# First feed-forward by halves, three more modulation vectors on TensorE, and the first two products of a stage side by side

## The chip, the cores and the metric

One core of a Trainium2 chip. The metric is the device time of one execution in microseconds; the median of the kernel before is 2867.61 us over 3 runs (2865.7 to 2867.91).

## The reference

A stack of two layers over 512 tokens `x` and 256 context tokens `ctx`, all 1024 wide. Each layer is a feed-forward, a mixer and a second feed-forward, each with a modulation computed from a condition vector. The mixer of layer 0 is attention with compressed keys beside an mLSTM, that of layer 1 a gated linear recurrence (RG-LRU).

```python
def ada_params(cond, w, b):
    m = jax.nn.silu(cond) @ w + b
    return jnp.split(m, N_MOD, axis=-1)          # 9 vectors of 1024
def modulate(h, shift, scale):
    return h * (1.0 + scale) + shift
def swiglu(h, w_gate, w_up, w_down):
    return (jax.nn.silu(h @ w_gate) * (h @ w_up)) @ w_down     # 1024 -> 2816 -> 1024

for layer in range(2):
    mx, mc = ada_params(c, ...), ada_params(c_ctx, ...)
    x = x + 0.5 * mx[2] * swiglu(modulate(rms_norm(x), mx[0], mx[1]), w_gate, w_up, w_down)
    ctx = ctx + 0.5 * mc[2] * swiglu(modulate(rms_norm(ctx), mc[0], mc[1]), ...)
    x, ctx = x + mx[5] * y_x, ctx + mc[5] * y_c      # y: even or odd mixer of the modulated norm
    x = x + 0.5 * mx[8] * swiglu(modulate(rms_norm(x), mx[6], mx[7]), ...)
    ctx = ctx + 0.5 * mc[8] * swiglu(modulate(rms_norm(ctx), mc[6], mc[7]), ...)    # layer 0 only
```

## The kernel before

**Layout.** The activations stay transposed in SBUF as eight tiles `xT[k]` of 128 features by 768 columns (256 of the context, 512 of x). An fp32 product is made of three products of parts: high by high, high by low, low by high. `split_to` writes a tile's high part (`xh`, `ah`) on ScalarE and its low part (`xl`, `al`) on VectorE (L522). The class `Stream` (object `ws`) loads weights into `raw` buffers and splits them into `unit` buffers, ScalarE for the high part (L260), VectorE for the low part (L261); three units are live at once.

**Stages.** P[0] to P[5] are the six stages: feed-forward, even mixer, feed-forward (layer 0), feed-forward, odd mixer, feed-forward (layer 1, x alone). The text calls them the first to the sixth. A `Normed` stage multiplies by the rms factor R only after its product. `chunk(k)` makes the stage's input for 128 features: `scale` (ScalarE L551 for `xh`, VectorE L552 for `xl`), then `square`, which squares on ScalarE (L562) and adds to `acc` (L563). That add runs on GpSimd for k below `SQ` (8; in the sixth stage `SQ3`, 6), else on VectorE. `chunk` is called by the stage before as soon as its last down product has been accumulated into `xT[k]` (L741). `shifts` puts the shift vectors into four extra columns (L522, tiles of 128x4). `norm` multiplies `acc` by ones on TensorE (`nps`, L584 and L585, in halved stages L718 and L719) and takes the root: `rv`, ScalarE's sqrt, a reciprocal (L514) and a Newton step to `ry`.

**Feed-forwards.** The hidden width is 22 blocks of 128, the f-blocks. `gen_ffn`, of the first stage, makes for each f-block two whole products of 48 matmuls (8 chunks, 3 part products, tiles of 258 and 512 columns; L598). `gen_halved`, of the third, fourth and sixth, makes the first 4 f-blocks so (`whole`) and the other 18 by a scheme of halves (`halves`): seven products of 12 matmuls of 386 columns (L730), after sums and differences of weights (`Stream`) and of inputs (`widen`, `settle`) on VectorE. The down products (L782, halved L908) come in groups of f-blocks, `HG` = 4, 4, 4, 4, 3, 3, two outputs side by side. Both functions yield after each product or so, and at each yield a `fill` function is called.

**Modulation.** The 9 vectors of layer 0 are numbered 0 to 8. Those in `order` (1, 0, 2) are made on TensorE in 12 steps of 256 columns: `mod_step` issues the loads of the next step, `mod_mm` (8 matmuls with the weights moving, L366) and `mod_post` of the step before (two transposes L377, then VectorE). The other vectors of both layers are made by `mod_late` on VectorE: per 768 columns and chunk a multiply-add of 128x768 (L465) into `macc`, then a transpose, a reduce and four small matmuls (L441). `mod_some(n)` advances it n operations per yield: 6.3 in the first stage (`MF0`), 0.4 and 0.52 in the third and fourth. `mod_ready` makes what is still missing before its use.

**Order.** The Tile framework's scheduler fixes each engine's order from the program; by hand only the start and first products (`ordered(OS)`) and ScalarE's order in the odd mixer. Each engine works in its order.

**Product starts.** In `gen_halved` with no `first`, `whole(0)` makes the gate product, yields, calls `norm`, then makes the up product. In the odd mixer `values(0)` (V0) makes its product and the norm, then `branch(0)` (B0) its own; `proj_start` of the even mixer makes the product of the gates and then that of `v`, head 0.

Of the kernel before, what the change touches and what calls it, by code (L numbers as in the profile page):

```python
# [15 lines left out]
KD = 8  # L16
# [25 lines left out]
SQ = 8  # L42
# [7 lines left out]
SQ3 = 6  # L50
# [37 lines left out]
FL = 2  # L88
FS = 2
MF0 = 6.3  # L90
MF1 = 0.4
MF2 = 0.52
HG = [4, 4, 4, 4, 3, 3]
# [4 lines left out]
NPX = 4  # L98


ALL = [(0, 258, [(0, 0, 256, C)], 256), (258, 770, [(0, 256, 768, X)], None)]
XO = [(256, 514, [(2, 256, 512, X)], 0), (514, 770, [(0, 512, 768, X)], None)]
# [19 lines left out]
def tile_hybrid_block(  # L122
# [188 lines left out]
    ws = Stream()  # L311
# [33 lines left out]
    order = [(0, 4 * n + i) for n in (1, 0, 2) for i in range(4)]  # L345
# [65 lines left out]
    def mod_late():  # L411
# [3 lines left out]
        todo = [(l, g, b, k) for l, g in ((0, 1), (0, 2), (1, 0), (1, 1), (1, 2)) for b in range(4) for k in range(KD)]  # L415
# [77 lines left out]
    def mod_ready(l, n):  # L493
        while MS["left"][l, n]:
            if (l, n // 3) == (0, 0):
                mod_step()
            else:
                next(MS["late"])
# [25 lines left out]
    class Normed:  # L524
# [78 lines left out]
        def part(self, u, ps, i):  # L603

            a, b, _, _ = self.tiles[i]
            todo = [(k, n) for k in range(KD) for n in range(3)]
            if PO:
                todo.sort(key=lambda q: q[1])
            for k, n in todo:
                wi, src = ((0, self.h), (0, self.lo), (1, self.h))[n]  # L610
                mm(ps[:, 0:b - a], lhsT=u[:, wi, k, :], rhs=src[k][:, a:b], start=(k, n) == (0, 0), stop=(k, n) == (KD - 1, 2))

# [181 lines left out]
    def gen_halved(P, l, j, nxt, first=None, plain=NP, groups=HG):  # L794
# [27 lines left out]
        def whole(f):  # L822
            if f == 0 and first is not None:
                pg, pu = first
            else:
                pg = P.product(ws.next())
                yield
                if f == 0:
                    P.norm()
                pu = P.product(ws.next())  # L830
# [281 lines left out]
    def proj_start(P):  # L1112

        pss = P.product(ws.next(), 64)
        M["z"], M["turn"] = {}, [[], []]
        first = gen_proj(P, [("v", 0)])
        next(first)
# [700 lines left out]
    def odd_mixer(P, nxt):  # L1818
# [26 lines left out]

        def values(n):
            pz = steps()
            if n == 0:
                P.norm()
            bz = P.bias(pz)  # L1850
# [32 lines left out]
        def branch(n):  # L1883
            pg = steps(XO)
# [111 lines left out]
    add_ffn(0, 0)  # L1996
# [10 lines left out]
    P = [Normed(0, 0), Normed(0, 1), Halved(0, 2), Halved(1, 0), Normed(1, 1), Halved(1, 2, True)]  # L2007
# [50 lines left out]
    def fill():  # L2058
        MS["n"] = MS.get("n", 0) + 1
        if MS["n"] < FS:  # L2060
            pass
        elif MS["mm"] <= len(order):
            mod_step(FL)
        else:
            some_late()
# [6 lines left out]
    run(gen_ffn(P[0], 0, 0, P[1].chunk, pss), fill)  # L2072
# [67 lines left out]
```

## Time and profile before

| | us |
|---|---|
| median of 3 runs | 2867.61 |
| profiled execution | 2867.53 |
| its span | 2865.8 |
| TensorE busy | 2756.6 (96%) |
| VectorE busy | 2229.0 (78%) |
| ScalarE busy | 1096.7 (38%) |
| GpSimd busy | 263.8 (9%) |

The span is the time from the first to the last instruction; the rest of the execution's time lies around it. Busy time says how long an engine had something to do and nothing of how fast it ran: TensorE's clock is granted in two levels, and the mean granted clock of a stretch stands beside its busy times.

### The profile page before, as it was taken

The page shows a single profiled execution, that of the slowest core. Times are in us where ns is not written, and L with a number is a line of the kernel's source. Part 1 is how long each engine was busy: PE and PEld are TensorE (multiplying, and loading weights), DVE is VectorE, ACT ScalarE, POOL GpSimd, SP SyncE. Part 2 cuts the span into 40 slices and gives each one's busy share as a digit, 9 for nine tenths or more (in the row PEclk, how much of TensorE's full clock was granted, in tenths as well). Part 3 has the DMA queues.
Part 4 walks back from the last instruction along what each step waited for, and adds up shares of the span by engine and source line. Part 5 has one row for each costly group of instructions (what it writes and reads, how often), then busy time and mean ns, then how long its engine had stood idle before and what let it go on. Part 6 is the DMA issues. An engine that isn't in the chain of part 4 may idle for free.

```text
span 2865.8 us, 40947 instructions
## 1 busy us (share of the span) xinstructions
PE 2756.6 (96%) x16185; PEld 2453.1 (86%) x16185; DVE 2229.0 (78%) x3673; ACT 1096.7 (38%) x1743; POOL 263.8 (9%) x274
## 2 busy tenths in 40 slices
PE   6999999999999899899999999999999997899998
PEld 4888888888888677789999998999999886799997
DVE  5367767796765667878879897989887899888886
ACT  4212111234443456443223344323323475643433
POOL 1000000021342200100000010000000353100000
PEclk8999999999999899999999999999999998899999
DMA  7434333342443110123223232234322211223332
GB/s 208 124 114 133 119 128 125 122 141 54 139 146 107 55 58 31 52 77 100 87 83 107 89 95 72 91 116 147 133 92 71 58 57 49 85 82 103 100 101 87
DMA packets 356634, 282.00 MB, mean 98 GB/s; under 512 B 14665, under 2 KB 327226, under 8 KB 356442
## 3 DMA queue, kind: packets, MB, share of 16 engines
q1 hardware_dynamic: 353722, 266.02, 30.1%
q0 software_dynamic: 2720, 13.37, 1.3%
q8 instruction: 127, 2.08, 0.3%
q14 instruction: 65, 0.53, 0.1%
HBM read 263.78 MB, written 15.56 MB: 97 GB/s over the span
## 4 chain that ended last, share of the span: by engine, by line
PE 54%; DVE 9%; issue 1%; ACT 1%; DMA 1%; POOL 0%; SPq 0%; DVEq 0%; ACTq 0%
PE ps L730 24%; PE ps L908 16%; PE ps L598 8%; PE ps L1416 2%; DVE xl L552 2%; DVE unit L261 1%; DVE xT L741 1%; PE oacc L1633 1%; PE ps L1590 1%; PE ps L1621 1%; DVE U L1873 1%; PE ps L1900 1%; DVE I L1931 0%; DVE S L1936 0%; DVE S L1929 0%
## 5 line engine op out<-in xcount | busy, mean ns | idle before, releaser
L598 PE MATMUL ps<-xh,unit 128*128 128x258 f32 (+3 forms) x3328 | 727.4, 337 | 10.5 <-DVE unit L261 8.7
L260 ACT CAST unit<-raw 128x1024 fp32r<-128x1024 f32 (+3 forms) x338 | 333.7, 988 | 943.7 <-PE ps L598 236.1
L598 PEld LDWEIGHTS ps<-xh,unit 128*128 128x128 f32 x3328 | 568.3, 193 | 77.8 <-DVE unit L261 10.1
L730 PE MATMUL ps<-xh,unit 128*128 128x386 f32 (+1 forms) x2592 | 617.6, 321 | 0.8 <-DVE g L804 0.7
L730 PEld LDWEIGHTS ps<-xh,unit 128*128 128x128 f32 x2592 | 451.6, 189 | 4.6 <-DVE g L804 1.5
L598 PE MATMUL ps<-xl,unit 128*128 128x258 f32 (+4 forms) x1664 | 425.6, 335 | 16.1 <-DVE xl L522 9.4
L261 DVE TENSOR_TENSOR unit<-raw,unit 128x1024 fp32r<-128x1024 f32 (+3 forms) x354 | 410.8, 1162 | 32.2 <-ACT unit L260 30.4
L908 PE MATMUL ps<-ah,unit 128*128 128x256 f32 (+1 forms) x1760 | 418.3, 349 | 2.5 <-ACT ah L521 2.5
L730 PE MATMUL ps<-xl,unit 128*128 128x386 f32 (+1 forms) x1296 | 414.1, 320 | 0.0
L598 PEld LDWEIGHTS ps<-xl,unit 128*128 128x128 f32 (+1 forms) x1664 | 311.1, 193 | 49.1 <-DVE xl L522 11.0
L908 PEld LDWEIGHTS ps<-ah,unit 128*128 128x128 f32 x1760 | 306.0, 188 | 48.6 <-ACT ah L521 4.5
L741 DVE SCALAR_TENSOR_TENSOR xT<-ps,mv,xT 128x256 f32<-128x256 f32 (+1 forms) x368 | 216.6, 633 | 74.3 <-PE ps L908 47.2
L908 PE MATMUL ps<-al,unit 128*128 128x256 f32 (+1 forms) x880 | 249.1, 349 | 0.0
L730 PEld LDWEIGHTS ps<-xl,unit 128*128 128x128 f32 x1296 | 244.7, 189 | 0.8
L465 DVE SCALAR_TENSOR_TENSOR macc<-mraw,csT,macc 128x768 f32<-128x768 f32 x245 | 241.0, 1017 | 2.0 <-DMA mraw<-in_mod_w_dram 1.9
L563 POOL TENSOR_TENSOR acc<-acc,sq 128x768 f32<-128x768 f32 (+1 forms) x33 | 65.2, 1975 | 1523.3 <-ACT sq L562 829.4
L908 PEld LDWEIGHTS ps<-al,unit 128*128 128x128 f32 x880 | 165.3, 188 | 23.4 <-DVE al L522 1.2
L626 DVE COPY bias<-ps 128x2 f32<-128x2 f32 (+1 forms) x82 | 12.7, 155 | 189.8 <-PE ps L598 186.5
L782 PE MATMUL ps<-ah,unit 128*128 128x256 f32 x704 | 152.8, 337 | 0.0
L782 PEld LDWEIGHTS ps<-ah,unit 128*128 128x128 f32 x704 | 120.1, 188 | 15.2
L521 ACT CAST ah<-u 128x768 fp32r<-128x768 f32 (+1 forms) x88 | 68.8, 782 | 112.5 <-DVE u L816 93.3
L730 PE MATMUL ps<-xh,four 128*128 128x386 f32 (+1 forms) x432 | 108.7, 320 | 0.0
(384 smaller groups left out, 3895.0 us busy)
## 6 DMA issues: line engine op xcount, KB each, us to landing
mraw<-in_mod_w_dram SPq DMA_DIRECT2D x184, 384.0 KB, 5.5
raw<-in_ffn_w_gate_dram SPq DMA_DIRECT2D x88, 512.0 KB, 3.9
raw<-in_ffn_w_up_dram SPq DMA_DIRECT2D x88, 512.0 KB, 3.9
raw<-in_ffn_w_down_dram SPq DMA_DIRECT2D x48, 512.0 KB, 3.6
raw<-in_ffn_w_down_dram SPq DMA_DIRECT2D x40, 384.0 KB, 3.2
raw<-in_even_w_in_dram SPq DMA_DIRECT2D x21, 512.0 KB, 5.1
raw<-in_odd_w_in_dram SPq DMA_DIRECT2D x16, 512.0 KB, 4.0
raw<-in_ffn_w_down_dram SPq DMA_DIRECT2D x16, 320.0 KB, 2.9
```

What stands on the lines that cost most here:

```text
L260: nc.scalar.copy(u[:, 0, 0:w], t)
L261: (nc.gpsimd if e == 2 else v).tensor_tensor(out=u[:, 1, 0:w], in0=t, in1=f(u[:, 0, 0:w]), op=ALU.subtract)
L465: v.scalar_tensor_tensor(out=o, in0=r[:, 0:768], scalar=s, in1=o, op0=ALU.mult, op1=ALU.add)
L521: nc.scalar.copy(hi, src)
L552: v.scalar_tensor_tensor(out=lo[:, a + o:b + o], in0=xT[k][:, a:b], scalar=s, in1=f(h[:, a + o:b + o]), op0=ALU.mult, op1=ALU.subtract)
L563: eng.tensor_tensor(out=self.acc[:, t], in0=self.acc[:, t], in1=sq[:, t], op=ALU.add)
L598: mm(ps[0:m, 0:b - a], lhsT=u[:, wi, k, 0:m], rhs=src[k][:, a:b], start=k == 0 and i == 0, stop=k == KD - 1 and i == 2)
L730: mm(ps[:, 0:H], lhsT=u[:, wi, o + k, :], rhs=src, start=start, stop=k == 3 and wi == 1, skip_group_check=True)
L741: v.scalar_tensor_tensor(out=xT[d][:, a:b], in0=ps[:, 0:b - a], scalar=mod_vec(l, n, d, j), in1=xT[d][:, a:b], op0=ALU.mult, op1=ALU.add)
L782: mm(ps[:, 0:b - a], lhsT=u[:, wi, q, :], rhs=src[:, a:b], start=q == 0 and i == 0, stop=q == G - 1 and i == 2)
L908: mm(ps[:, 0:c.stop - c.start], lhsT=us[n][:, wi, q, :], rhs=src[:, c], start=q == 0 and i == 0, stop=q == G - 1 and i == 2)
L1416: mm(ps[:, 0:b - a], lhsT=u[:, wi, q, o:o + 128], rhs=src[:, a:b], start=q == 0 and i == 0, stop=q == len(ys) - 1 and i == 2)
```

## The change

1. The first stage becomes a `Halved` stage: `add_halved(0, 0, NP0)` for its weights, `gen_halved` with 4 whole f-blocks for its work; its first two products come, as before, from `first`.
2. `order` gets the vectors 7, 6 and 8 of layer 0, 12 more steps on TensorE, and `mod_late` loses them. `fill` makes the first steps at every second yield, and the others one by one, each 14th yield (`MP`); `MF0` goes from 6.3 to 0.5.
3. `SQ` and `SQ3` become 0: all adds of squares run on VectorE.
4. `HG` becomes 4, 4, 4, 3, 3, 4 (the sixth stage keeps its own list).
5. `together` makes the first two products of a stage side by side, in turns of two chunks, and the norm comes behind both; `proj_start` does the same for its two products.

```diff
-SQ = 8
+SQ = 0
-SQ3 = 6
+SQ3 = 0
-MF0 = 6.3
+MF0 = 0.5
-HG = [4, 4, 4, 4, 3, 3]
+HG = [4, 4, 4, 3, 3, 4]
+NP0 = 4
+MP = 14
+FP = 1
...
-    order = [(0, 4 * n + i) for n in (1, 0, 2) for i in range(4)]
+    order = [(0, 4 * n + i) for n in (1, 0, 2, 7, 6, 8) for i in range(4)]
...
-        todo = [(l, g, b, k) for l, g in ((0, 1), (0, 2), (1, 0), (1, 1), (1, 2)) for b in range(4) for k in range(KD)]
+        todo = [(l, g, b, k) for l, g in ((0, 1), (1, 0), (1, 1), (1, 2)) for b in range(4) for k in range(KD)]
...
-            if (l, n // 3) == (0, 0):
+            if (l, n // 3) in ((0, 0), (0, 2)):
                 mod_step()
...
+        def together(self, us, tiles=(None, None)):
+            out = [[] for _ in us]
+            left = [self.product_steps(u, o, tiles=t) for u, o, t in zip(us, out, tiles)]
+            while left:
+                left = [g for g in left if next(g, g) is not g]
+            return out
...
         def whole(f):
-            if f == 0 and first is not None:
-                pg, pu = first
+            if f == 0:
+                pg, pu = first or P.together([ws.next(), ws.next()])
+                if first is None:
+                    P.norm()
+                yield
             else:
                 pg = P.product(ws.next())
                 yield
-                if f == 0:
-                    P.norm()
                 pu = P.product(ws.next())
...
-        pss = P.product(ws.next(), 64)
+        pss = []
+        gates = P.product_steps(ws.next(), pss, 64)
         M["z"], M["turn"] = {}, [[], []]
         first = gen_proj(P, [("v", 0)])
-        next(first)
+        for _ in range(3):
+            next(gates)
+            next(first)
+        run(gates)
         P.norm()
...
         def values(n):
-            pz = steps()
             if n == 0:
+                early.extend(P.together([ws.next(), ws.next()], (None, XO)))
                 P.norm()
+            pz = steps() if n else early[0]
...
-            pg = steps(XO)
+            pg = steps(XO) if n else early[1]
...
-    add_ffn(0, 0)
+    add_halved(0, 0, NP0)
...
-    P = [Normed(0, 0), Normed(0, 1), Halved(0, 2), Halved(1, 0), Normed(1, 1), Halved(1, 2, True)]
+    P = [Halved(0, 0), Normed(0, 1), Halved(0, 2), Halved(1, 0), Normed(1, 1), Halved(1, 2, True)]
...
     def fill():
-        MS["n"] = MS.get("n", 0) + 1
-        if MS["n"] < FS:
+        n = MS["n"] = MS.get("n", 0) + 1
+        if n < FS:
             pass
-        elif MS["mm"] <= len(order):
-            mod_step(FL)
+        elif MS["posted"] < 12:
+            if n % 2 == FP:
+                mod_step(FL)
         else:
+            if n % MP == 0:
+                mod_step(1)
             some_late()
...
-    run(gen_ffn(P[0], 0, 0, P[1].chunk, pss), fill)
+    run(gen_halved(P[0], 0, 0, P[1].chunk, pss, NP0), fill)
```

**TensorE at the start of the third stage.** `unit_10632` holds the weights of its first product, `ps_10860` and `ps_10861` are that product's tiles of 260 and 512 columns. Before, all of the product comes first, chunk after chunk (here the first three chunks):

```order
L598 MATMUL ps_10860<-xh_10651,unit_10632 128x260
L598 MATMUL ps_10861<-xh_10651,unit_10632 128x512
L598 MATMUL ps_10860<-xl_10652,unit_10632 128x260
L598 MATMUL ps_10861<-xl_10652,unit_10632 128x512
...
L598 MATMUL ps_10860<-xh_10675,unit_10632 128x260
L598 MATMUL ps_10861<-xh_10675,unit_10632 128x512
L598 MATMUL ps_10861<-xl_10676,unit_10632 128x512
...
L598 MATMUL ps_10861<-xh_10700,unit_10632 128x512
L598 MATMUL ps_10861<-xl_10701,unit_10632 128x512
```

Now `unit_10741` and `unit_10845` are the first and the second product:

```order
L601 MATMUL ps_10974<-xh_10760,unit_10741 128x260
L601 MATMUL ps_10975<-xh_10760,unit_10741 128x512
...
L601 MATMUL ps_10975<-xl_10785,unit_10741 128x512
L601 MATMUL ps_10975<-xh_10784,unit_10741 128x512
L601 MATMUL ps_10988<-xh_10760,unit_10845 128x260
L601 MATMUL ps_10988<-xl_10761,unit_10845 128x260
...
L601 MATMUL ps_10989<-xl_10785,unit_10845 128x512
L601 MATMUL ps_10989<-xh_10784,unit_10845 128x512
L601 MATMUL ps_10975<-xh_10809,unit_10741 128x512
L601 MATMUL ps_10975<-xl_10810,unit_10741 128x512
```

After two chunks of the first product the same two chunks of the second follow, before the first goes on to the third chunk.

**VectorE at the end of the second stage**, where the last chunks of the third stage's input are made. Before:

```order
L741 SCALAR_TENSOR_TENSOR xT6_78<-ps_10790,mv0_96,xT6_78 128x512
L552 SCALAR_TENSOR_TENSOR xl_10806<-xT6_78,mv0_96,xh_10805 128x256
L741 SCALAR_TENSOR_TENSOR xT7_79<-ps_10814,mv0_96,xT7_79 128x256
L741 SCALAR_TENSOR_TENSOR xT7_79<-ps_10815,mv0_96,xT7_79 128x512
L552 SCALAR_TENSOR_TENSOR xl_10806<-xT6_78,mv0_96,xh_10805 128x512
L522 TENSOR_TENSOR xl_10676<-mv0_96,xh_10675 128x4
```

Now:

```order
L752 SCALAR_TENSOR_TENSOR xT7_79<-ps_10924,mv0_96,xT7_79 128x512
L566 TENSOR_TENSOR acc_10766<-acc_10766,sq_10920 128x768
L555 SCALAR_TENSOR_TENSOR xl_10940<-xT7_79,mv0_96,xh_10939 128x256
L555 SCALAR_TENSOR_TENSOR xl_10940<-xT7_79,mv0_96,xh_10939 128x512
L566 TENSOR_TENSOR acc_10766<-acc_10766,sq_10945 128x768
L525 TENSOR_TENSOR xl_10785<-mv0_96,xh_10784 128x4
```

The adds to `acc` (L566, the old L563) now stand among the low parts, and the 128x4 tiles of the shifts behind the last add.

**TensorE at the start of the fifth stage.** Before, `unit_19837` is V0 and `unit_19904` is B0:

```order
L598 MATMUL ps_20013<-xh_19960,unit_19837 128x258
L598 MATMUL ps_20014<-xh_19960,unit_19837 128x512
L584 MATMUL nps_20075<-ah_20071,ones_85 128x384
L584 MATMUL nps_20078<-ah_20071,ones_85 128x384
L598 MATMUL ps_20103<-xh_19749,unit_19904 128x258
L598 MATMUL ps_20104<-xh_19749,unit_19904 128x256
L598 MATMUL ps_20103<-xl_19750,unit_19904 128x258
L585 MATMUL nps_20075<-al_20072,ones_85 128x384
```

Now `unit_19966` is V0, `unit_20046` B0 and `unit_20177` the product after them:

```order
L601 MATMUL ps_20186<-xh_20118,unit_19966 128x512
L601 MATMUL ps_20199<-xh_20107,unit_20046 128x258
...
L601 MATMUL ps_20199<-xh_20118,unit_20046 128x258
L601 MATMUL ps_20200<-xh_20118,unit_20046 128x256
L587 MATMUL nps_20289<-ah_20285,ones_85 128x384
L588 MATMUL nps_20289<-al_20286,ones_85 128x384
L601 MATMUL ps_20334<-xh_19853,unit_20177 128x258
```

The norm's matmuls moved from behind the first product to behind both.

## Rows read from the trace of the kernel before

**Rows 1.** The page's first part: busy us, share of the span, instructions.

```profile
PE 2756.6 (96%) x16185; PEld 2453.1 (86%) x16185; DVE 2229.0 (78%) x3673; ACT 1096.7 (38%) x1743; POOL 263.8 (9%) x274
```

**Rows 2.** Busy times by stretch, first stage to sixth; columns in the first line.

```profile
core 0: us, PE busy (x) PEld busy (x) DVE busy (x) ACT busy (x) POOL busy (x), PEclk, DMA share, GB/s
72.40:622.60 550.20, 549.33 (x3218) 476.64 (x3217) 372.84 (x551) 123.02 (x169) 10.27 (x5) 1.00 0.39 125
622.60:646.60 24.00, 20.83 (x103) 15.75 (x102) 22.24 (x34) 7.46 (x12) 6.21 (x5) 0.86 0.53 136
1187.20:1214.30 27.10, 19.90 (x103) 17.17 (x102) 24.77 (x30) 12.24 (x19) 7.74 (x5) 0.87 0.19 55
1214.30:1718.60 504.30, 504.30 (x2889) 472.99 (x2888) 428.92 (x629) 174.51 (x238) 7.04 (x4) 1.00 0.29 91
1718.60:1743.30 24.70, 20.92 (x103) 17.67 (x102) 22.72 (x23) 9.54 (x15) 7.45 (x5) 0.86 0.26 80
2248.10:2271.80 23.70, 18.78 (x101) 16.46 (x101) 22.78 (x37) 12.04 (x19) 8.95 (x5) 0.86 0.16 45
2492.10:2510.50 18.40, 14.57 (x101) 14.32 (x101) 16.46 (x23) 8.85 (x15) 3.88 (x4) 0.81 0.29 86
```

**Rows 3.** The same view: whole products (first stage), then halves (third stage).

```profile
231.70:333.60 101.90, 101.90 (x591) 89.20 (x584) 64.40 (x97) 22.53 (x29) 0.00 (x0) 1.00 0.34 111
1298.60:1358.35 59.75, 59.75 (x345) 59.17 (x344) 49.98 (x73) 22.50 (x29) 0.00 (x0) 1.00 0.36 113
```

**Rows 4.** Timeline of TensorE, two modulation steps: start, us, instruction, records, idle before.

```profile
90.73 0.63 PE L366 MATMUL mps<-mraw,csT 128*32 128x256 f32 x6 [0.68 <-DMA mraw<-in_mod_w_dram]
109.25 1.07 PE L366 MATMUL mps<-mraw,csT 128*32 128x256 f32 x16
110.44 0.60 PE L598 MATMUL ps<-xh,unit 128*128 128x258 f32 x2
```

**Rows 5.** Waits at the starts of stages 2, 3, 4, 6: us, times, longest.

```profile
PE ps L598 <- DVE unit L261: 3.2, 1, 3.2
PE ps L598 <- DVE xl L522: 6.3, 1, 6.3
PE ps L598 <- DVE xl L552: 2.8, 1, 2.8
PE ps L598 <- DVE xl L552: 3.8, 1, 3.8
```

**Rows 6.** Timeline of VectorE (DVE) and GpSimd (POOL): kernel start, then third stage.

```profile
12.52 0.95 DVE L563 TENSOR_TENSOR acc<-acc,sq 128x768 f32<-128x768 f32 x1
1189.04 0.75 DVE L552 SCALAR_TENSOR_TENSOR xl<-xT,mv,xh 128x512 fp32r<-128x512 f32 x1
1192.34 2.12 DVE L552 SCALAR_TENSOR_TENSOR xl<-xT,mv,xh 128x512 fp32r<-128x512 f32 x1
1197.16 3.73 DVE L522 TENSOR_TENSOR xl<-mv,xh 128x4 fp32r<-128x4 f32 x5
1192.10 1.82 POOL L563 TENSOR_TENSOR acc<-acc,sq 128x768 f32<-128x768 f32 x1 [0.35 <-ACT sq L562]
```

**Rows 7.** Timeline, third stage: the norm's first matmul, first product scaled.

```profile
1205.05 0.34 PE L718 MATMUL nps<-ah,ones 128*128 128x384 f32 x1
1217.85 1.03 DVE L834 TENSOR_TENSOR g<-ps,ry 128x260 f32<-128x260 f32 x2
```

**Rows 8.** Timeline of TensorE, fifth stage: norm and first gate product.

```profile
2264.56 1.01 PE L585 MATMUL nps<-al,ones 128*128 128x384 f32 x2 [1.09 <-DVE al L522]
2286.11 0.51 PE L1900 MATMUL ps<-uh,unit 128*128 128x256 f32 x2
```

**Rows 9.** Timeline of TensorE, second stage, after its first products.

```profile
668.10 1.29 PE L1137 MATMUL ps<-ident,zv 128*128 128x128 f32 x3 [4.40 <-ACT zv L1175]
```

**Rows 10.** The page's costliest groups (late modulation) and its DMA issues.

```profile
L465 DVE SCALAR_TENSOR_TENSOR macc<-mraw,csT,macc 128x768 f32<-128x768 f32 x245 | 241.0, 1017 | 2.0 <-DMA mraw<-in_mod_w_dram 1.9
mraw<-in_mod_w_dram SPq DMA_DIRECT2D x184, 384.0 KB, 5.5
```

More of the change, by code (lines that the diff above doesn't have):

```diff
@@ L1844, in ticks @@
                 tick()
+        early = []
         def values(n):
-            pz = steps()
             if n == 0:
+                early.extend(P.together([ws.next(), ws.next()], (None, XO)))
                 P.norm()
+            pz = steps() if n else early[0]
             bz = P.bias(pz)
```

## The prediction

> **What bounds the kernel now.** The page first: TensorE is busy for 2756.6 of 2865.8 us [rows 1], so time is saved only by giving it fewer matmuls or by closing the gaps between them. The busy time by stage [rows 2] tells which of the two is possible where. In the first feed-forward, from the third product on (72.4 to 622.6), TensorE works 549.33 of 550.20 us: nothing to close there, only matmuls to remove. The halved feed-forward of the third stage needs 504.30 us for the same stretch of its own work, TensorE busy throughout, with VectorE at 85% (428.92 of 504.30). The gaps lie in the few us in which a stage starts: 24.0, 27.1, 24.7, 23.7 and 18.4 us up to the third product, at granted clocks of 0.81 to 0.87 where the stages around them have 1.00. The reader is to see two numbers in each start: how much TensorE idled, and how far the clock, which has the levels 1.2 and 2.4 GHz here, was down for part of the rest. The waits [rows 5] tell on what: always on VectorE, mostly for the low part `xl` of a late chunk. The profiled execution took 2867.53 us, 1.7 more than its span and 0.1 less than the median of the runs, 2867.61; the sum is made against 2867.5.
>
> **First feed-forward by halves.** Afterwards this stage is the program of the third stage: the same 22 f-blocks, 4 whole and 18 by halves, the same down products, and TensorE was never short of work there. So I take its 504.3 us [rows 2] and add what it has besides. That is 16 modulation steps, 4 that stood there before and 12 new ones. One takes from 109.25, where its 16 records begin, to 110.44, where the next product begins: 1.2 us [rows 4]. 16 x 1.2 = 19.2, and 1.5 us for the small matmuls that the late modulation leaves in this stage. 504.3 + 19.2 + 1.5 = 525.0, against 550.2: **-25.2 us**. A second way: per halved f-block 84 matmuls stand for 96, so 18 x 12 = 216 go; one costs 59.75 / 336 = 177.8 ns among halves and 101.9 / 576 = 176.9 ns among whole products [rows 3] (336 and 576 are 4 and 6 f-blocks' worth by the program; the records hold a few more or fewer). 216 x 0.1778 = 38.4, less 12 x 1.2 = 14.4: -24.0. The two agree; the bounds: the first step of this stage also waited for its transfer, 0.68 us [rows 4], so 1.9 a step, 30 for 16 and a gain of only 14; below, the 16 records alone take 1.07, which makes 17 for 16 and 2 us more gain. I take 1.2, the later steps' price, since the transfers are issued a step ahead, 14 yields before use.
>
> VectorE, which in this stage was busy for 372.84 of 550.20, gets the sums and the subtractions of the halves, but loses half of the late modulation: 80 multiply-adds of 128x768 instead of 160, by the program. Against the third stage it has 16 more of these (80 to 64) at 1.01 [rows 10]: 428.9 + 16 = 445 of 525, again 85%. Priced at nothing: what hides it is TensorE's own 100%; uncovered it would be those 16 us, less the idle time.
>
> **The adds of squares go from GpSimd to VectorE**, 7 each at the starts of five stages. One costs 0.95 us on VectorE [rows 6]. On GpSimd it cost no issue there, but in the row at 1192.34 the `xl` of 512 columns beside such an add (1192.10, 1.82 us) took 2.12, where the same operation took 0.75 at 1189.04: +1.4. Worse, five tiny operations of 128x4 took 3.73 us at 1197.16, beside two adds, and the 6.3 us wait of TensorE [rows 5] ends on them. So each moved add gives VectorE 1.4 back for 0.95: about +0.4 us an add, and the pile at the end is gone. The Trainium skill, SBUF — State Buffer, section "Who interferes with whom", says that the port pair shared by VectorE and GpSimd is an exclusive lock, so that the loser stands still: by it an add costs VectorE its whole 1.82 rather than 1.4, five of them 2.1 us more in the third stage's start, and the sum would be -52.4 instead of -50.7.
>
> **Side by side, and a last group of 4.** Before, the first product of a stage needs all eight chunks within its 8.5 us, while VectorE needs some 3.2 for one: 0.75 for 512 columns of `xl` [rows 6], half of it again for 256, as much for the residual's accumulation, and the add. Now two products share each chunk, so TensorE has 17 us of work for eight chunks; and the last down group of 4 f-blocks gives VectorE 48 x 0.177 = 8.5 us for each pair of chunks, of which it needs 2 x 3.2. When the stage starts six chunks stand ready, 12.8 us of work, and the last two are done some 7 us in. So the waits should go. The floor of a start is 96 x 0.1778 = 17.1 plus 0.35 of the norm's own matmuls: 17.4. What is above it: second stage 24.0 - 17.4 = 6.6, third 27.1 - 17.4 = 9.7, fourth 24.7 - 17.4 = 7.3. I take **-6.5, -8 and -7**: nearly all, since VectorE's need is well below the time given, and a little less in the third, whose tail is the longest. The bounds are 3 (only the waits of [rows 5] in the second and fourth) to 11 (with some of the later stall below). In the last stage TensorE idles 18.4 - 14.57 = 3.8, and the clock of 0.81 costs its work 0.19 x 14.57 = 2.8: **-4**, bounds 2 and 6.5.
>
> **The fifth stage: nothing.** There the products side by side put the norm's matmuls behind both products, where they stood behind the first. But what TensorE does at 2286.11, the gate products, waits for the root, its reciprocal, the convolution and a split, a chain that begins with the norm at 2264.56 [rows 8]: 21.5 us. If TensorE comes sooner to the norm by the waits it loses, and later by the second product, the chain starts about when it did. 0, bounds -3 and +5. In the second stage the wait of 4.40 at 668.10 for `zv` [rows 9] is likewise left as it is: VectorE still has the bias of the next product ahead of the scaling.
>
> **Sum:** -25.2 - 6.5 - 8 - 7 + 0 - 4 = -50.7; 2867.5 - 50.7 = 2816.8, so **2817 us**.
>
> **Rivals.**
> (1) The root, not the chunks, sets the starts. From the norm's matmul at 1205.05 to the first scaled product at 1217.85 it takes 12.8 us [rows 7]. Now the norm stands behind both products, at start + 17, so banks come free at start + 30, and the fifth product wants one at start + 34. The margin is 4 us where it was 13. For it: VectorE has adds ahead in its queue. Against: 4 us is still a margin. It decides from 4 us of delay; half of the 25.5 us of the starts is lost, +13: 2830. Chance 0.2.
> (2) The stalls left alone above go too, since their inputs come earlier: 4.4 at 668.10 and some 5 of the fifth stage: 2867.5 - 60 = 2807. Against: both are chains through the root. Chance 0.15.
> (3) VectorE becomes the bound. In the fourth stage it gets some 24 more operations of about 1.01 us [rows 10] for modulation that the first stage no longer does, and 7 adds at 0.95: 428.9 (as in the third stage) + 24 + 7 = 460 of 504.3, 91%. If none of the 24 to 33 us fits into its idle time, 2841 to 2850. Against: at 85% it held up nothing. It decides once VectorE's idle time of 75 us isn't usable. Chance 0.1. The Trainium skill, Perfetto Trace Analysis, section "Optimizing Scalar/DVE Operations", advises to move work off a saturated VectorE, even to GpSimd, which speaks against this change's adds; it also warns that the two share a port, and the trace bears that half out (+1.4 us above).
> (4) Slower: each of the 12 new steps stops TensorE, in order, for its own transfer. The median from issue to landing is 5.5 us [rows 10], 6.2 with the step's tail: 12 x 6.2 = 74, so 2891. It decides from 50.7 / 12 = 4.2 us a step. For it: the first step of the stage did wait, 0.68 [rows 4]. Against: transfers are issued a step ahead. Chance 0.03.
>
> **How the numbers follow.** The forecast has 0.52, the rivals 0.2, 0.15, 0.1 and 0.03. The range reaches from rival 2 with some of its bounds, 2804, to rival 1 with some of a dearer step, 2836; (3) and (4) lie outside. About 0.2% (5.7 us) is what a measurement of this kernel can tell from no change: only (4), or (3) at several times its price, comes near. Faster 0.95, same 0.02, slower 0.03.
>
> **What would show it.** Right: first stage from its third product about 525 us with TensorE full; no wait of TensorE over 1 us in the starts of stages two, three, four and six, clocks of 0.95 or more there, each start 17 to 19 us; `xl` at 0.75 throughout; the gate products of the fifth stage at the same distance from its start. Wrong: modulation steps with a wait for `mraw` before them; TensorE waiting on VectorE inside the fourth stage; the fifth product of a stage waiting for a bank.

## The result, and the profile after

The changed kernel takes 2817.19 us (median of 4 runs, 2813.15 to 2817.88) beside 2866.65 us of the kernel before: ratio 0.9825, 95% interval 0.9808 to 0.9842. Forecast were 2817, with 2804 to 2836 as the range. The profiled execution took 2817.39 us, 50.1 less than that of before.

The table has the length of each stage in the profiled executions, from its first product to that of the next, read off the timelines of TensorE (the labels of the experiments stand in the next section). The experiments ran on several chips, on which the kernel before took 2866.65 to 2870.37 us, and one kernel's executions differ by up to some 9 us (e8): differences of medians of a few us are not read as such below, and each row of stages is one execution.

| run | to the 1st stage's third product | 1st | 2nd | 3rd | 4th | 5th | 6th | median |
|---|---|---|---|---|---|---|---|---|
| before | 72.5 | 550.2 | 564.5 | 531.4 | 529.5 | 244.0 | 373.6 | 2866.7 |
| after | 71.8 | 528.8 | 557.5 | 522.1 | 522.9 | 242.6 | 369.9 | 2817.2 |
| e1 adds on GpSimd | 73.4 | 527.9 | 556.5 | 532.5 | 522.5 | 243.6 | 371.9 | 2830.8 |
| e9 third stage's adds on VectorE | 72.8 | 528.5 | 559.2 | 522.8 | 522.7 | 242.8 | 371.7 | 2821.6 |
| e3 groups back | 73.1 | 527.5 | 553.9 | 521.6 | 523.0 | 243.1 | 369.2 | 2818.7 |
| e2 products in turn | 71.3 | 539.6 | 550.4 | 528.4 | 523.8 | 237.1 | 372.4 | 2825.2 |
| e10 in turn, same fill | 72.1 | 528.3 | 550.8 | 528.3 | 522.1 | 235.2 | 372.4 | 2810.1 |
| e6 norm earlier | 72.3 | 529.0 | 558.3 | 522.5 | 524.8 | 238.1 | 368.9 | 2815.7 |
| e7 mixers in turn | 72.1 | 528.4 | 551.3 | 522.4 | 522.7 | 237.5 | 368.8 | 2804.9 |
| e4 first stage alone | 71.9 | 528.9 | 565.2 | 531.2 | 533.5 | 247.2 | 372.5 | 2852.8 |
| e8 starts alone | 72.6 | 549.7 | 566.6 | 521.4 | 522.8 | 238.2 | 370.4 | 2843.5 |
| e5 vectors on VectorE | 72.1 | 558.6 | 562.2 | 522.5 | 523.5 | 238.9 | 369.9 | 2848.7 |

By stages the change gave 0.7 + 21.4 + 7.0 + 9.3 + 6.6 + 1.4 + 3.7 = 50.1 us. The busy times of the changed kernel by stretch answer to [rows 2]; columns as there (length, PE, PEld, DVE, ACT, POOL busy, granted clock, DMA):

```profile
71.80:600.60 528.80, 527.75 (x3177) 483.70 (x3176) 446.58 (x693) 179.21 (x256) 2.14 (x3) 1.00 0.41 126
600.60:618.20 17.60, 17.60 (x101) 14.32 (x100) 12.05 (x21) 8.50 (x14) 0.00 (x0) 1.00 0.40 99
1158.10:1175.80 17.70, 17.70 (x104) 15.60 (x103) 13.92 (x27) 10.09 (x18) 0.00 (x0) 1.00 0.20 58
1175.80:1680.20 504.40, 504.40 (x2890) 473.77 (x2889) 436.44 (x642) 177.18 (x243) 0.11 (x1) 1.00 0.29 92
1680.20:1697.80 17.60, 17.60 (x103) 15.56 (x102) 11.53 (x18) 6.65 (x10) 0.00 (x0) 1.00 0.16 53
1697.80:2203.20 505.40, 505.40 (x2915) 474.46 (x2915) 450.18 (x656) 175.54 (x241) 1.73 (x6) 1.00 0.35 112
2203.20:2236.40 33.20, 29.41 (x197) 27.08 (x195) 27.68 (x62) 11.65 (x18) 4.57 (x5) 0.99 0.17 48
2236.40:2252.10 15.70, 15.65 (x73) 13.60 (x74) 12.21 (x19) 14.19 (x18) 9.65 (x6) 0.80 0.30 86
2445.80:2459.10 13.30, 12.26 (x101) 12.06 (x100) 11.19 (x23) 7.79 (x15) 0.00 (x0) 1.00 0.24 70
```

The reader is to see: the starts of the second, third and fourth stage, up to the third product (rows 2, 3, 5), are 17.6 to 17.7 us long, TensorE busy in all of it at a clock of 1.00, where they took 24.0, 27.1 and 24.7 at 0.86 and 0.87 [rows 2]. That is the floor of 17.4 that the prediction named, plus 0.2 to 0.3. The first stage takes 528.8, not 525.0. VectorE in it is busy for 446.6 (forecast 445), in the fourth for 450.2 of 505.4, 89%, and TensorE loses nothing there. The fifth stage's start (row 7) ends in a wait, and behind it (row 8) the clock is 0.80.

What TensorE still waited for in the first 60 us of the second stage, and in the first 47 of the fifth (us in all, times, longest):

```profile
PE ps L1153 <- ACT zv L1191: 3.5, 2, 1.9
...
PE ps L1919 <- ACT uh L1896: 3.8, 1, 3.8
```

Both hang on the root: the value tiles `zv` and the convolved input `uh` are scaled by it. And two modulation steps of the first stage, on TensorE's timeline as in [rows 4]:

```profile
81.36 0.63 PE L369 MATMUL mps<-mraw,csT 128*32 128x256 f32 x6 [1.05 <-DMA mraw<-in_mod_w_dram]
...
100.01 0.52 PE L601 MATMUL ps<-xh,unit 128*128 128x260 f32 x2
100.46 1.07 PE L369 MATMUL mps<-mraw,csT 128*32 128x256 f32 x16
101.46 0.44 PE L380 MATMUL mps<-ident,msb 128*128 128x128 f32 x2
101.65 0.60 PE L601 MATMUL ps<-xh,unit 128*128 128x260 f32 x2
```

The second of the two matmuls that begin at 100.01 starts some 0.13 later; it would be followed after 0.18 by the next, which comes at 101.65. Measured so, from the last matmul before a step to the first after it less one matmul's 0.18, a step costs 1.28 to 1.35 us, and the first one, cut in three and with a wait for its transfer, 3.2. All modulation on TensorE in this stage comes to 24.5 us.

### The profile page after: what moved, and what is told of

The parts are those of the page before. It is cut to its first block, busy times and chain, and to the rows that moved or that the text cites. A ratio compares the mean times of both kernels' runs of the same rounds, so it can differ in the third digit from the quotient of the medians.

```text
span 2815.7 us, 41074 instructions
## 1 busy us (share of the span) xinstructions
PE 2728.8 (97%) x16155; PEld 2457.8 (87%) x16155; DVE 2295.2 (82%) x3848; ACT 1151.1 (41%) x1829; POOL 204.3 (7%) x242
## 4 chain that ended last, share of the span: by engine, by line
PE 88%; DVE 7%; DMA 1%; SPq 1%; issue 1%; ACT 1%; POOL 0%; DVEq 0%; ACTq 0%; POOLq 0%
PE ps L741 34%; PE ps L920 24%; PE ps L601 16%; PE ps L1432 3%; PE num L1281 1%; PE ps L1606 1%; DVE unit L264 1%; PE oacc L1649 1%; PE ps L1637 1%; PE ps L1258 1%; DVE U L1892 1%; PE ps L1919 1%; PE mps L369 1%; PE ps L1520 1%; SPq L357 1%
## 5 line engine op out<-in xcount | busy, mean ns | idle before, releaser
L741 PE MATMUL ps<-xh,unit 128*128 128x386 f32 (+1 forms) x3456 | 848.2, 326 | 0.4
L741 PEld LDWEIGHTS ps<-xh,unit 128*128 128x128 f32 x3456 | 610.7, 189 | 4.1 <-DVE g L815 1.0
L920 PE MATMUL ps<-ah,unit 128*128 128x512 f32 (+1 forms) x2464 | 573.8, 347 | 2.5 <-ACT ah L524 2.5
L741 PE MATMUL ps<-xl,unit 128*128 128x386 f32 (+1 forms) x1728 | 561.2, 325 | 0.0
L601 PE MATMUL ps<-xh,unit 128*128 128x258 f32 (+5 forms) x2176 | 468.7, 331 | 6.4 <-DVE unit L264 5.4
L601 PEld LDWEIGHTS ps<-xh,unit 128*128 128x128 f32 (+1 forms) x2176 | 363.6, 190 | 46.9 <-DVE unit L264 6.3
L741 PEld LDWEIGHTS ps<-xl,unit 128*128 128x128 f32 x1728 | 327.0, 189 | 1.2
L752 DVE SCALAR_TENSOR_TENSOR xT<-ps,mv,xT 128x512 f32<-128x512 f32 (+1 forms) x400 | 233.2, 632 | 76.9 <-PE ps L920 58.2
L601 PE MATMUL ps<-xl,unit 128*128 128x258 f32 (+2 forms) x1088 | 274.2, 327 | 0.0
L601 PEld LDWEIGHTS ps<-xl,unit 128*128 128x128 f32 x1088 | 199.2, 190 | 18.2
L815 DVE TENSOR_TENSOR u<-ps,u 128x386 f32<-128x386 f32 (+1 forms) x216 | 112.4, 520 | 38.9 <-PE ps L741 37.9
```

The source lines that it names most:

```text
L601: mm(ps[0:m, 0:b - a], lhsT=u[:, wi, k, 0:m], rhs=src[k][:, a:b], start=k == 0 and i == 0, stop=k == KD - 1 and i == 2)
L741: mm(ps[:, 0:H], lhsT=u[:, wi, o + k, :], rhs=src, start=start, stop=k == 3 and wi == 1, skip_group_check=True)
L752: v.scalar_tensor_tensor(out=xT[d][:, a:b], in0=ps[:, 0:b - a], scalar=mod_vec(l, n, d, j), in1=xT[d][:, a:b], op0=ALU.mult, op1=ALU.add)
L815: v.tensor_tensor(out=out, in0=ps[:, 0:H], in1=more, op=ALU.add)
L920: mm(ps[:, 0:c.stop - c.start], lhsT=us[n][:, wi, q, :], rhs=src[:, c], start=q == 0 and i == 0, stop=q == G - 1 and i == 2)
```

## The experiments

**e1 and e9: where the adds of squares run.** Own theory: an add on VectorE frees it of more than it costs, but side by side hides most of that. Rivals: the adds alone made the starts short, or their place is worth nothing.

```diff
-SQ = 0
-SQ3 = 0
+SQ = 8
+SQ3 = 6
```

> The changed kernel with one part undone: the adds of squares run on GpSimd again (28 of 768 columns and 5 of the sixth stage's 7). Own theory: beside such an add an operation of VectorE takes about 1.4 us longer, against 0.95 for the add itself, and the tiny operations on the shift columns end later; but the two products side by side leave a margin of some us at each start, so TensorE waits only a little. 2820 us (2817 to 2826), xl of 512 columns at 2 us again beside an add, each start longer by under 2 us. Rival A, the adds were what made the starts short: the waits of 3 to 6 us come back in four starts, 2832 to 2840. Rival B, the adds' place is worth nothing once the products stand side by side: 2817, starts of the third and fourth stage 17.6 to 17.8 as now.

Measured: 2830.78 us (ratio to before 0.9868, 0.9854 to 0.9881), 13.6 more than the changed kernel: above the own range, just short of rival A's. The table shows that neither has the place right: 10.4 us of it lie in the third stage alone and 2.0 in the sixth. The starts of the second and the fourth stage stay at 17.6 and 17.7; that of the fifth takes 17.9 instead of 15.0, but the stage is only 1.0 longer. The third stage's start in e1 by busy times, as above:

```profile
1157.80:1184.90 27.10, 20.23 (x104) 17.12 (x103) 18.39 (x27) 10.71 (x18) 7.70 (x5) 0.87 0.11 33
```

VectorE and GpSimd on its timeline there:

```profile
1162.89 2.12 DVE L555 SCALAR_TENSOR_TENSOR xl<-xT,mv,xh 128x512 fp32r<-128x512 f32 x1
1167.70 3.76 DVE L525 TENSOR_TENSOR xl<-mv,xh 128x4 fp32r<-128x4 f32 x5
...
1162.64 1.82 POOL L566 TENSOR_TENSOR acc<-acc,sq 128x768 f32<-128x768 f32 x1 [0.35 <-ACT sq L565]
1167.31 4.06 POOL L566 TENSOR_TENSOR acc<-acc,sq 128x768 f32<-128x768 f32 x2 [2.84 <-ACT sq L565]
```

And TensorE's longest wait in it:

```profile
PE ps L601 <- DVE xl L525: 6.0, 1, 6.0
```

In the changed kernel seven of those tiny operations take 0.59 us:

```profile
1168.52 0.59 DVE L525 TENSOR_TENSOR xl<-mv,xh 128x4 fp32r<-128x4 f32 x7
```

So five operations that need some 0.4 us last 3.76 beside two adds of 4.06. Record by record, three of the five take 0.15 each and the other two 1.79 and 1.83, and these two end 0.02 us after the two adds. TensorE's wait of 6.0 us ends on them, with a lower clock after it. The 3.3 us that they lose are only a part of that wait: the chunks before them came late too. The start is 27.1 us long, as before the change [rows 2], products side by side or not. To see whether that one place is the whole of it, e9 leaves only the third stage's adds on VectorE:

```diff
-            self.square(k, v if k >= (SQ3 if self.l and self.n == 2 else SQ) else nc.gpsimd)
+            self.square(k, v if (self.l, self.n) == (0, 2) else nc.gpsimd)
```

> The changed kernel with the adds of squares on VectorE only for the third stage's input, on GpSimd for all other stages. Own theory: in the run with all adds on GpSimd 10.4 of the 12.6 us lost in its trace lie in the third stage, where five tiny operations on the shift columns took 3.76 us beside two adds and TensorE waited 6.0 us on them, and 2 in the sixth; the chunks come fastest there, at the even mixer's end. So this gives most of it back: 2819 us (2817 to 2822), tiny operations of the third stage 0.6 us in all. Rival, each start gains a little from its adds (those at the other starts take 1.4 us a piece): 2824 or more.

Measured: 2821.57 us (0.9839, 0.9825 to 0.9852), in the own range: 9.2 of the 13.6 us are the third stage's, whose start is 17.7 again. About 4 us stay, which the intervals of the two kernels don't separate; 1.8 of them lie in the sixth stage, as in e1, the others are spread over stages in a way that two profiles differ by anyway. The pair shows that the adds matter at the even mixer's end and little elsewhere. There the chunks come faster: in the changed kernel the eight `xl` of 512 columns end within 21.0 us, those of the second, fourth and fifth stage within 26.5 to 27.8. That this is why is argued, not shown.

The Trainium skill, SBUF — State Buffer, section "Who interferes with whom", calls the port pair of the two engines an exclusive lock. The runs agree: the two long operations of four columns end 0.02 us after the adds beside them, and what VectorE loses is near the length of the add (3.3 of 4.06, and 2.12 less 0.74, 1.4, of 1.82).

**e3: the last down group.**

```diff
-HG = [4, 4, 4, 3, 3, 4]
+HG = [4, 4, 4, 4, 3, 3]
```

> The changed kernel with one part undone: the down groups are 4, 4, 4, 4, 3, 3 again, the last with 3 f-blocks. Own theory: a pair of chunks then has 36 x 0.177 = 6.4 us instead of 8.5, VectorE needs about 6.5 with the adds, so it is a us or two behind at a start, inside the margin of the two products side by side: 2818 us (2816 to 2822), starts of the third and fourth stage at 17.6 to 18.5. Rival, the group of 4 is what gave VectorE its time: waits of 2 to 5 us in three starts, 2825 to 2833.

Measured: 2818.65 us (0.9824, 0.981 to 0.9837): no difference, starts of the third and fourth stage at 17.7. The fifth stage's start is longer (18.5 to its third product instead of 15.0), but its length is the same. The rival falls: with products side by side and the adds on VectorE the order of the groups is worth nothing measurable.

**e2 and e10: first products in turn.** The whole of side by side is undone, in the feed-forwards and in both mixers:

```diff
-            if f == 0:
-                pg, pu = first or P.together([ws.next(), ws.next()])
-                if first is None:
-                    P.norm()
-                yield
+            if f == 0 and first is not None:
+                pg, pu = first
             else:
                 pg = P.product(ws.next())
                 yield
+                if f == 0:
+                    P.norm()
                 pu = P.product(ws.next())
...
```

> The changed kernel with one part undone: the first two products of a stage come one after the other and the norm stands behind the first (all of the side by side part taken back, also in the two mixers). Own theory: the first product needs the last two chunks 6.4 us after the start and the shift columns soon after, VectorE is done with them some 7.3 us after it: waits of 1 to 3 us and a lower clock behind them in four starts, +4 to +12; against that the norm comes 8.5 us earlier, which takes away the waits for the root at the second stage's value tiles (3.5 us) and at the fifth stage's gates (3.8 us and a lower clock behind it), -3 to -8. 2819 us (2812 to 2826). Rival, side by side is what closed the starts: 25 us lost, 2838 to 2842.

Measured: 2825.21 us (0.985, 0.9836 to 0.9863), in the own range, but for a reason that was not in it. The second and fifth stage became 7.1 and 5.5 us shorter, the third and sixth 6.3 and 2.5 longer, and the first 10.8 longer, where nothing had been meant to change. A step of the modulation waited there for its transfer:

```profile
95.92 1.08 PE L369 MATMUL mps<-mraw,csT 128*32 128x256 f32 x6 [7.75 <-DMA mraw<-in_mod_w_dram]
97.69 2.23 PE L369 MATMUL mps<-mraw,csT 128*32 128x256 f32 x10 [0.70 <-DMA mraw<-in_mod_w_dram]
```

The edit had also taken away one yield of the first stage's first f-block, and with it moved every step to another yield: TensorE came to this step at 88.2, but its loads were issued from 91.72 on, behind two loads of down weights that held SyncE's queue from 82.13. In the changed kernel they are issued at 75.24, ahead of those. e10 is e2 with that yield:

```diff
                 pg, pu = first
+                yield
```

> The kernel with all first products in turn once more, now with the first f-block of the first stage yielding as in the changed kernel, so that the modulation steps fall on the same yields. Own theory: the wait of 7.7 us for a transfer of modulation weights in that run, and 10.8 us of its first stage in all, came from the steps falling on other yields (step right behind its load) and not from the products: first stage 529 us, total 2825.2 - 10.8 = 2814.4 (2812 to 2818). Rival, products in turn cost the first stage itself something: 2822 to 2826.

Measured: 2810.06 us (0.9805, 0.9791 to 0.9819), below the range: first stage 528.3, as expected. With all products in turn the kernel is 7 us faster than the changed one by the medians, though the two intervals overlap a little. The stages say it more plainly: the second and fifth are 6.7 and 7.4 us shorter, the third and sixth 6.2 and 2.5 longer, and the fourth's start is 17.7 either way. So side by side as a whole loses, though it does what it was thought to do in the third and sixth stage.

**e6: the norm earlier in the mixers.** If the root is what the mixers wait for, an earlier norm should help without giving up side by side:

```diff
+                norm -= 1
+                if not norm:
+                    self.norm()
                 left = [g for g in left if next(g, g) is not g]
...
-                early.extend(P.together([ws.next(), ws.next()], (None, XO)))
-                P.norm()
+                early.extend(P.together([ws.next(), ws.next()], (None, XO), 4))
...
+        P.norm()
         run(gates)
-        P.norm()
```

> The changed kernel with the norm's matmuls put earlier in the two mixers: ahead of the last two chunks of the first two products (12 matmuls earlier in the second stage, 20 in the fifth). Own theory: what still makes TensorE wait there is the chain from the norm over the root (value tiles in the second stage 3.5 us, gate products in the fifth 3.8 us and half clock behind it). The low part of the sum of squares is there in time (610.2 and 214 ns past 2213 in the changed kernel's trace, norm now at 615.4 and 2217.4), so the chain starts 2 us earlier in the second and 3 us earlier in the fifth: 2812 us (2809 to 2815). Rival A, the wait is not the root's but a split or a bias in VectorE's order: 2817. Rival B, the low part of the sum comes too late and TensorE waits at the norm instead: 2817 to 2822.

Measured: 2815.70 us (0.9818, 0.9804 to 0.9831), a little above the own range, and not to be told from the changed kernel. The fifth stage did get 4.5 us shorter, its wait for `uh` fell from 3.8 to 1.5. The second did not: one of its two waits for `zv` went, and another took its place. That is neither rival's: rival B had TensorE wait at the norm, and this wait is for a sum of squares of the mixer that GpSimd adds.

```profile
PE ps L1156 <- ACT zv L1194: 1.9, 1, 1.9
PE ssc L1164 <- POOL sq L1205: 1.6, 1, 1.6
```

**e7: side by side in the feed-forwards alone.** Only the edits in `proj_start`, `values` and `branch` are taken back:

```diff
-        gates = P.product_steps(ws.next(), pss, 64)
+        pss = P.product(ws.next(), 64)
...
-        for _ in range(3):
-            next(gates)
-            next(first)
-        run(gates)
+        next(first)
         P.norm()
...
+            pz = steps()
             if n == 0:
-                early.extend(P.together([ws.next(), ws.next()], (None, XO)))
                 P.norm()
-            pz = steps() if n else early[0]
...
-            pg = steps(XO) if n else early[1]
+            pg = steps(XO)
```

> The changed kernel with the first two products side by side in the halved feed-forwards alone; in both mixers they come in turn and the norm stands behind the first, as before the change. Own theory: in the run with all products in turn the second stage was 7.1 us and the fifth 5.5 us shorter than in the changed kernel, because the chain of the root starts earlier there and TensorE waits for it there; the third and sixth, where the chunks are late, were 6.3 and 2.5 us longer. So the mixers' part of side by side costs 12.6 us: 2804.6 (2802 to 2809). Rival A, what made those two stages shorter in that run was its late first stage (VectorE had time to get ahead): 2815 to 2818. Rival B, as in the run with the norm alone earlier, the chain moves and the next wait takes its place: 2813 to 2816.

Measured: 2804.87 us (2804.81 to 2805.0; 0.9773, 0.976 to 0.9786). That is 12.3 us below the changed kernel, with intervals that don't meet, and as forecast: second stage 551.3 instead of 557.5, fifth 237.5 instead of 242.6. Both rivals fall: the gain is there with the first stage as in the changed kernel. It is clear of what one profile differs from another by: behind the first stage by halves the second stage is 550.4 to 551.3 us in the three runs in turn (e2, e10, e7) and 553.9 to 559.2 in the five side by side (after, e1, e9, e3, e6). The second stage has no wait of TensorE over its first 60 us, and in the first 53 of the fifth the wait for `uh` is gone too; what is left there is

```profile
PE ps L601 <- DVE xl L525: 0.9, 1, 0.9
```

The second stage's start is as short as with side by side (row 1; the others are the third and the sixth stage's):

```profile
600.60:618.20 17.60, 17.60 (x102) 14.30 (x101) 16.52 (x21) 9.09 (x14) 0.00 (x0) 1.00 0.50 128
1151.80:1169.40 17.60, 17.60 (x103) 15.50 (x102) 13.84 (x27) 10.01 (x18) 0.00 (x0) 1.00 0.19 57
2434.50:2447.80 13.30, 12.28 (x102) 12.08 (x101) 11.17 (x23) 7.84 (x15) 0.00 (x0) 1.00 0.25 74
```

In e10, with these in turn too, the third and the sixth stage start like this:

```profile
1151.30:1174.70 23.40, 20.29 (x104) 16.60 (x103) 20.88 (x31) 11.56 (x19) 0.00 (x0) 0.93 0.22 63
2436.90:2454.80 17.90, 14.74 (x102) 13.54 (x101) 16.03 (x26) 9.68 (x16) 0.00 (x0) 0.90 0.30 88
```

There side by side takes 5.8 and 4.6 us off the starts. e7 is the best version of the study.

**e4 and e8: do the terms add up?** e4 is the kernel before with the first stage by halves and the three vectors on TensorE:

```diff
-SQ = 0
-SQ3 = 0
-HG = [4, 4, 4, 3, 3, 4]
+SQ = 8
+SQ3 = 6
+HG = [4, 4, 4, 4, 3, 3]
```

with the products in turn as in e10. e8 is the rest of the change, with the first stage as before.

> The kernel before with the first stage by halves and the three more vectors on TensorE, and nothing else of the change: adds on GpSimd, groups 4, 4, 4, 4, 3, 3, first products in turn everywhere. Own theory, the terms add up: the first stage gave 21.4 us in the changed kernel's trace (550.2 to 528.8, of which 24.5 are modulation on TensorE), the starts are those of before: 2846 us (2843 to 2850). Rival, the first stage's gain is tied to the rest (VectorE, at 85% there, needs the starts to be short, or the adds on GpSimd stop it inside the stage): 2852 or more.

> The changed kernel with the first stage as before (whole products, three vectors on TensorE, the others on VectorE at the old pace); adds, groups and products side by side as in the change. Own theory, the terms add up: 50.1 - 21.4 = 28.7 us less than before: 2839 us (2836 to 2842). Rival, the first stage's form sets part of the second stage's start too: 2843 or more.

Measured: 2852.78 us (0.9942, 0.9929 to 0.9954) and 2843.48 us (0.9911, 0.9896 to 0.9926), beside 2870.37 of before on that chip. So 17.6 and 26.9 us, 44.5 together, where the change gives about 50. Both rivals' times came out; by the medians alone that gap is hardly clear of the intervals, but the table says where it lies: the second stage is 565.2 and 566.6 us, no shorter than before in either, and 557.5 with both parts. The reason that e4's rival gave does not hold, since the first stage is 528.9 there, the same as in the changed kernel; but the starts of the fourth and the fifth stage are longer than before (27.1 and 26.1 instead of 24.7 and 23.7). In the fifth one a transpose and a reduce of the late modulation stand between the chunks on VectorE, beside adds on GpSimd; the fourth stage's trace has 78 late multiply-adds instead of 56. That these lengthen the starts is argued and not shown. In e8 the second stage's start stays at 23.95 us instead of 17.6, though the adds are on VectorE and the products side by side: TensorE still waits, perhaps because whole down products hand over the chunks in another rhythm, which no run isolates:

```profile
PE ps L601 <- DVE xl L525: 2.2, 1, 2.2
PE ps L601 <- DVE unit L264: 2.1, 1, 2.1
```

So of the second stage's gain most needs the first stage by halves as well.

**e5: are the three vectors right on TensorE?** They go back to the late modulation, at 1.1 operations a yield.

```diff
-MF0 = 0.5
+MF0 = 1.1
...
-    order = [(0, 4 * n + i) for n in (1, 0, 2, 7, 6, 8) for i in range(4)]
+    order = [(0, 4 * n + i) for n in (1, 0, 2) for i in range(4)]
...
```

> The changed kernel with the vectors 7, 6 and 8 made by the late modulation on VectorE again (1.1 operations a yield in the first stage instead of 0.5), so 12 steps fewer on TensorE. Own theory: TensorE saves 12 x 1.33 = 16 us, to 513, but VectorE, busy for 446.6 of 528.8 in the first stage, gets 86 multiply-adds of 1.01 and 16 transposes and reduces of 0.95 more: 549 us, more than TensorE has; the first stage takes 540 to 555 and VectorE becomes its bound: 2833 us (2825 to 2845). Rival, what doesn't fit moves into the second stage, where VectorE has room, and TensorE gets its 16 us back: 2801 to 2805.

Measured: 2848.66 us (0.9925, 0.9913 to 0.9938), 31.5 more than the changed kernel, with the first stage at 558.6: past the own range, and the opposite of the rival. VectorE is busy for 93% of nearly the whole stage on average (row 1), but for 97% of it from 172 us on (row 2):

```profile
72.00:615.00 543.00, 513.66 (x2913) 474.20 (x2911) 506.05 (x736) 164.88 (x226) 0.00 (x0) 0.97 0.39 127
172.00:615.00 443.00, 413.96 (x2310) 389.06 (x2308) 431.40 (x610) 126.66 (x168) 0.00 (x0) 0.97 0.38 125
```

TensorE's longest waits up to the second stage's start:

```profile
PE ps L741 <- DVE g L815: 18.6, 7, 4.2
PE ps L920 <- ACT unit L263: 4.3, 2, 2.2
PE ps L741 <- DVE u L815: 3.1, 2, 1.7
```

All of TensorE's 29 us of waiting but the first few tenths lie in row 2, 24 of them on VectorE. The average of 93% hides that: in the first 100 us, where TensorE waits 0.3, VectorE is at 75%. Nor is 93% a limit. In the changed kernel the end of the first and of the fourth stage have VectorE at 96 and 94%, and TensorE loses nothing:

```profile
522.00:600.00 78.00, 78.00 (x452) 73.67 (x451) 74.98 (x117) 34.55 (x55) 2.14 (x3) 1.00 0.37 102
2097.80:2203.20 105.40, 105.40 (x613) 99.29 (x612) 98.67 (x144) 40.39 (x62) 1.18 (x2) 1.00 0.36 118
```

So VectorE is the bound of e5's first stage, as its own theory had it, and it shows in TensorE's waits and not in a share. The 12 steps cost TensorE 12 x 1.33 = 16 us; they save these 29 and what the lower clock of the stretch (0.97) costs, so that the stage is 29.8 us shorter with them.

## Why the prediction was right, and which terms were not

**First stage: -25.2 forecast, -21.4 measured.** The mechanism was right: TensorE full, 504.3 us of halves, plus the modulation. Too small by 3.8 was the term "16 x 1.2 = 19.2, and 1.5". The step had been read in [rows 4] from its first record to the next product; the 0.13 between the last product and the step belongs to it. 15 steps at 1.33, one of 3.2 with a wait for its transfer, and the small matmuls are 24.5, and 504.3 + 24.5 = 528.8.

**Starts of the second, third, fourth and sixth stage: -25.5 forecast, -26.6 by stages.** "So the waits should go" held: the longest is 1.0 us, in the sixth, and the clock is 1.00. By stages -7.0, -9.3, -6.6 and -3.7 were measured for -6.5, -8, -7 and -4. But the parts had been bundled, and undone one at a time they show only some of their worth: the adds 13.6 (10.4 in the third stage, 2.0 in the sixth), side by side 5.8 and 4.6 at the starts of the third and sixth, the group of 4 nothing beside the other two. The starts of the second and the fourth stage stay at 17.6 to 17.7 whichever of the three is undone (e1, e10, e3), and take 25.3 and 27.1 with none of them (e4). So any two do there, no run has one alone, and these stages' 7.0 and 6.6 us can't be given to a part. The price "about +0.4 us an add" was far too small for the third stage: the tiny operations, caught beside two adds, ended the long wait. The prediction saw them ("the pile at the end is gone") but put no price on it. By the program 33 adds moved, 28 and 5 in the sixth stage, not 7 in each of five. And the sum with the lock's price would be 50.7 + 2.1 = 52.8, not 52.4.

**Fifth stage: 0 forecast, -1.4 measured.** "The chain starts about when it did" was wrong by some 2 us: the norm's matmuls start 14.3 us after the stage's start in both, but before their low parts came only 16.4 us after it (a wait of 1.1 for the low part of the sum), and now they follow at once; and the gate products come at 33.3 instead of 38.0. But now TensorE gets there first and waits 3.8 us, and the gate products that follow run at a clock of 0.80, until the next gate products 15.6 us instead of 12.7. So 4.7 gained and 2.9 given back. The stage's length does not follow its gate products alone: in e3 they come at 37.5 and the stage is 0.5 longer, in e8 at 33.3 too and it is 4.4 shorter. What makes that difference in the later parts, some 4 us against e5 and e8, stays open: those two have fewer late operations in the fourth stage (56 instead of 77), which is argued and not shown as the cause.

**The total.** That 2817 was met to 0.2 us is luck: the first stage gave 3.8 us less than forecast, the starts 1.1, the fifth stage 1.4 and the time up to the third product 0.7 more.

**The rivals.** (1) The root at the starts of the feed-forwards: no wait for a bank there; but the same mechanism held in both mixers, and there the change lost 12.3 us of what it could have had (e7). The prediction had seen the stall at `zv` and taken it as given; it was set by where the norm stands. (2) The stalls did not go by themselves, as it had it; they go with the norm behind the first product again, in e7, at 2804.87 where 2807 had been named. (3) VectorE at 89% in the fourth stage (forecast 91) held up nothing; e5 shows the case, in the first stage. The Trainium skill, Perfetto Trace Analysis, section "Optimizing Scalar/DVE Operations", says that moving work from a saturated VectorE to GpSimd may make sense, and that it might not help, since the two share a port. e1 bears out the second half: with the adds on GpSimd the kernel is 13.6 us slower. (4) A step that waits for its transfer cost 7.75 us once in e2, so the mechanism exists; there the loads were issued some 3.5 us after TensorE was ready for the step.

## What to carry to other kernels

Side by side helps where inputs arrive late and costs where the chain behind the norm is what the next work waits for: decide it per stage, by which wait ends last there. An operation of four columns can stand still as long as the GpSimd operation beside it, here 1.8 us twice, and a wait of TensorE of 6.0 us ended on such operations: look for tiny operations with long durations. The busy share of an engine beside a full TensorE does not tell whether it is the bound: a stage's 93% was 75% in its first 100 us and 97% after it, with 29 us of waits there, and stretches at 94 and 96% elsewhere cost nothing. Look at TensorE's waits in the stretch. And undoing one part of a change at a time shows nothing of parts that can stand in for each other: two starts here stayed short whichever part was undone.

## What the runs showed of the hardware that was not expected

Five VectorE operations of 128x4 lasted 3.76 us beside two GpSimd adds of 4.06 in all, two of the five 1.79 and 1.83, each to 0.02 us past the end of an add; seven of them alone took 0.59. After a wait of 3.8 us TensorE's granted clock was 0.80 over the next 15.7 us (row 8 above), where the same products had run at 1.00 in the kernel before, which came to them without a wait: that gave back more than half of what the shorter start had gained.
